# A hybrid GLA and attention step on one core: half a query tile and one gate in every head

## The chip, the core and the metric

The kernel runs on one NeuronCore of a Trainium2 chip. A core has engines that run beside each other, each with an instruction stream of its own: TensorE (PE, matrix products into PSUM), VectorE (DVE), ScalarE (ACT), GpSimd (POOL) and SyncE (SP, which here only issues DMAs). They wait for each other by semaphores, and 16 DMA engines move the data. The metric is the device time of one execution in microseconds (us); less is better.

## What is computed

One step of a two-layer backbone: layer 0 is bidirectional gated linear attention (GLA), layer 1 softmax attention with 8 query heads, 2 key/value heads and head size 128. There are 256 context tokens, which see only themselves, and 1024 latent tokens, which see all latent tokens and 256 cached context keys. The part around the change:

```python
def attn_project(h, w_in, qn, kn):
    proj = h @ w_in
    q, k, v, gate = jnp.split(proj, [ATT_QD, ATT_QD + ATT_KD, ATT_QD + 2 * ATT_KD], axis=-1)
    q = rms_norm(q.reshape(B, T, ATT_HEADS, HEAD_DIM), qn)
    ...
    def one(qblk):
        s = jnp.einsum("bqhgd,bkhd->bhgqk", qblk, keys).astype(jnp.float32) * scale
        p = jax.nn.softmax(s, axis=-1).astype(vals.dtype)
        return jnp.einsum("bhgqk,bkhd->bqhgd", p, vals)
...
        out_p = (attend_blocks(qp, kp, vp) * jax.nn.silu(gp)) @ att_w_out[i]
        ...
        xp = xp + gt_p * out_p
        xs = xs + gt_s * out_s
```

Before each layer, `h` is the RMS-normed residual stream, scaled and shifted by the conditioning; queries and keys of latent tokens get a rotary position.

## The kernel before

Every float32 product is made of two float16 parts (hi and lo) of each operand: `mm3` (L122) issues three matmuls, hi·hi, hi·lo and lo·hi, for each of the 8 blocks of 128 of the inner dimension. The 1280 tokens are 10 tiles of 128. One tile context holds the whole kernel; a scheduler in it, which simulates the engines, puts the instructions of each engine into an order of its own, close to that of the program; `issue_after(x)` says that what stands in the block comes after `x` in it.

The phases in the profiled execution are: GLA until about 557 us; the output of the GLA layer and the way into attention ("crossing") to about 736; attention to about 1177; its output projection to the end.

**Crossing**, `gla_out` (L849). For n = 2 to 9 (tiles in the order 4 to 9, then 0 and 1; two were done in the GLA phase) it makes `y = o @ w_out` into PSUM, adds it to the residual rows `x` (`residual`), and normalises, modulates and splits them (`mod_tile`, which ends with transposing DMAs into `hT_hi`, `hT_lo`, the stationary operand of the attention projections). `out_load` (L827) loads a tile of the GLA output (`og`), `out_prep` (L835) splits it into hi and lo (`oghl`) and transposes it by two DMAs that SP issues (L844, L845) into the tile's own columns of `hT_hi` and `hT_lo`, from which the matmuls of `y` read it until `mod_tile` writes there. Keys and values of attention are made beside it (`key_tile`, tile name `kv`). At n = 4 the query weights (`whi2`) are loaded by SP (L909), and at n = 8 and 9 the first two query tiles are made (`query`, `query_rest`). SP issues in order, so a transposing DMA stands behind what was issued before. PREP (L40) are slots of the GLA phase in which the first four tiles are loaded and prepared, EARLY those in which the first two are made.

**Attention**, `attention` (L1205). There are 10 steps, a pair of a key/value head p and a chunk c of 256 tokens, and 4 query heads in each, 40 heads in all. In the two steps of c = 0 (n = 4 and 6) there are 256 keys ("small"), in all others 1280 ("large"). For a head and each half j of the chunk:

- `scores` (L1091): S = q·kT into one of two PSUM tiles `S` of 3 banks (L1104, 9 matmuls for 1280 keys), its row maximum `smx` on DVE (L1107), `snb` on ACT (L1109), and p = exp on ACT (L1112), after which the bank is free.
- `rest` (L1118): the reciprocal of the sum (`srec` L1128, `srec2`), then p is normalised and split into one `phl` tile: hi on POOL for j = 0 (L1134), on ACT for j = 1 (L1136), lo on DVE (L1137). A transposing DMA by SP (L1138) takes it to `PT`. `phl` has two buffers, `PT` three.
- `gateT` (L1141): the head's gate, 24 matmuls 256 wide into a bank `mm`, emptied by ACT, then SiLU.
- `values` (L1151): v·PT, 30 matmuls for a large head, into a bank `mm`; DVE multiplies by the gate (L1162), POOL issues the store (L1163).

Queries (`queries`, L1063) are made a tile of 128 tokens and 512 columns (the four heads of p) at a time, ahead of their step: `query` (L1193) issues 24 matmuls 512 wide into a bank `mm`, takes them out by two ACT copies and finishes the norm, rotary position and transpose of two heads (`queries_out`); `query_rest` (L1201) does the other two. `mm` has two banks, shared by gates, queries, values and, at the start, `key_tile`. The queries' tiles `qT` lie in one of the two buffers `wst` of a pool for weights under way (which is why S reads `wst`); the other holds nothing in attention until the output of step n = 9 is loaded (`out2_load`, L1257).

The order of the program is: an even head makes S(j=0), a query tile, `rest`, S(j=1), and the values of the head two before; an odd head makes S(j=0), `query_rest`, values, S(j=1), then the gates of the even head and of itself, and `rest`.

**Behind it**, `out2_prep` (L1262, with `wmx`) and `out_tile` (L1280, through `residual` with banks of S) make the output projection, `fold_gate` (L807) scales its gate rows on POOL.

Of the kernel before, what the change touches and what calls it, by code (L numbers as in the profile page):

```python
# [17 lines left out]
P = 128  # L18
D = 1024
KT = D // P  # L20
TP, TS = 256, 1024
# [3 lines left out]
PAST = 256  # L25
# [13 lines left out]

PREP = (42, 44, 46, 48)  # L40
EARLY = (45, 47)
# [12 lines left out]
class K:  # L54
# [69 lines left out]
    def mm3(self, out, lhs, rhs, n=KT):  # L124
        for k in range(n):
            lh, ll = lhs(k)
            rh, rl = rhs(k)
            for j, (a, b) in enumerate(((lh, rh), (lh, rl), (ll, rh))):
                self.nc.tensor.matmul(out, a, b, start=k == 0 and j == 0, stop=k == n - 1 and j == 2)  # L129

# [695 lines left out]

    def out_load(self, i, og=None, parts=None):  # L827
        if og is None:
            og = self.og[:, i % 2]
            t = self.t(self.xp, [P, 2 * D], F16, "oghl", bufs=2)  # L830
            parts = t[:, 0:D], t[:, D:]
        self.nc.sync.dma_start(og, self.og_d[i])
        return i, og, parts
# [15 lines left out]
    def gla_out(self, wo, early, n0):  # L849
# [15 lines left out]
        for n in range(len(early), n0 + 4):  # L865
            rows[n] = self.out_load(order[n])
        ckv = self.att_load()
        for n in range(n0, NT):
            i = order[n]
            if n == NT - 1:  # L870
                self.query_rest()
                self.query()
                self.key_tile(order[n - 2], wkv)
                self.query_rest()
# [17 lines left out]
            if n == 8:  # L892
                self.query()
            if n == n0:
# [223 lines left out]
    def rest(self, after=None):  # L1118
# [11 lines left out]
        nc.vector.tensor_scalar(r2, r, 2.0 ** 14, None, ALU.mult)  # L1130
        parts = self.t(self.sp, [P, 2 * (TS + PAST)], F16, "phl")[:, 0 : 2 * nk]
        hi, lo = parts[:, 0:nk], parts[:, nk:]
# [51 lines left out]
    def query_low(self):  # L1184
# [6 lines left out]
        self.wg = [self.load_w("g0", (0, 2))]  # L1191

    def query(self):  # L1193
        if self.todo:
            p, c, j = self.todo.pop(0)
            t = self.queries(2 * c + j, *self.wq[p])
            self.half.append(t)
            self.q[(p, c, j)] = t[2]
            self.queries_out(t, 0)
# [5 lines left out]
    def attention(self, wo, wk):  # L1205
        self.S0, self.put_off = self.t(self.ps, [P, 1536], F32, "S"), None
        wq, wg, q, g = self.wq, self.wg, self.q, {}
        pend, later = [], []
        t = self.t(self.sp, [P, 20, 256], F16, "PT", bufs=3)[:, 0:16, :].rearrange("p (j k) n -> p j k n", j=2)
# [3 lines left out]
        for n, (p, c) in enumerate(self.steps):  # L1213
# [8 lines left out]
            for e in range(4):  # L1222
# [4 lines left out]
                self.scores(h, c, 0, q[(p, c, 0)], PT)  # L1227
                if e % 2 == 0:
                    self.query()
                    self.rest()  # L1230
                    self.scores(h, c, 1, q[(p, c, 1)], PT)
                else:
                    self.query_rest()
                if len(pend) == 2:
                    self.values(*pend[0], g.pop(pend.pop(0)[0]))
                else:
                    self.key_tile(len(pend), wkv)
                if e % 2 == 1:
                    self.scores(h, c, 1, q[(p, c, 1)], PT)
                pend.append((h, c, PT))  # L1240
                if e % 2 == 1:
                    g.update({i: self.gateT(i, c, *wg[p]) for i in (h - 1, h)})
                    self.rest()
                if n == 9 and e == 0:
                    row = self.out2_load(OUT[0])
                if n == 9 and e == 1:
                    first = self.ropet.rearrange("p a b d -> p (a b d)").bitcast(F16)
                    first = first.rearrange("p (j h t) -> p j h t", j=2, h=AH)
                    with self.tc.issue_after(self.last):
                        self.prep = self.out2_prep(row, (first[:, 0], first[:, 1]))  # L1250
        self.fold_gate(*self.gate_load(1), wo[0][2] + wo[1][2])
        wo[:] = [(hi, lo, 512) for hi, lo, _ in wo]
# [369 lines left out]
```

## Time and profile before

| | us |
|---|---|
| median of 3 runs | 1309.43 (1306.7 to 1311.03) |
| profiled execution | 1308.64 |
| its span | 1306.6 |
| mean granted clock of TensorE | 0.983 of full speed |
| PE idle between 560 and 1307, by the waits that ended it | 37.9 |

A page of the profile gives busy time, share of the span and number of instructions of each engine. The windows view gives the same for chosen stretches: the stretch, its length, busy time of PE, PEld (weight loads), DVE, ACT and POOL with the number of instructions in brackets, the granted clock, the share of the 16 DMA engines, GB/s. The waits view gives groups of waits of one engine: line waiting, `<-` the instruction that ended it, the sum in us, how often, the longest. A timeline row gives start, duration, engine, line, operation, result `<-` operands, sizes, and in brackets the idle time before it with what ended it; a matmul's row may stand for several in sequence (`x9`), and its duration reaches over the next one's start, so lengths are taken from start to start. Rows of SP (`SPq`) are the issuing of DMAs: how long SP stood at it, not when the data landed.

### The profile page before, as it was taken

Reading aid. Unit: us, or ns where it says so; the run is one execution under the profiler, and the core shown is the slowest. Engines: PE = TensorE matmul, PEld = TensorE weight load, DVE = VectorE, ACT = ScalarE, POOL = GpSimd, SP = SyncE. Lnnn points to the kernel's source line nnn. Section 1 sums busy time; section 2 is a strip of 40 time slices with the busy share of each in tenths; the row PEclk is TensorE's granted clock in tenths of the full one; section 3 lists DMA queues with packets and bytes.
Section 4 is the critical chain, followed back from the end, with each engine's and each line's share of the span. In section 5 each row is a group of like instructions: output and inputs, shape, how many; then the busy total and the mean of one; then the engine's idle time right before and its main releaser. Section 6 shows DMA issues by size and latency. Waiting matters only on the chain. (4 is left out here: it accounts for less than half of the span.)

```text
span 1306.6 us, 22246 instructions
## 1 busy us (share of the span) xinstructions
PE 1215.6 (93%) x7936; PEld 783.7 (60%) x7936; DVE 924.6 (71%) x2120; ACT 705.4 (54%) x1706; POOL 360.7 (28%) x594
## 2 busy tenths in 40 slices
PE   3899999999998989796999989999998999989998
PEld 2366666555645556574777557667665767766444
DVE  5575879877876798676776767777767587785652
ACT  3684656565655566541333376766766686673110
POOL 1132214223321143410223334342232345322000
PEclk9899999999998999998999999999999999999999
DMA  9712655554646343269956597666957648879342
GB/s 359 251 33 82 211 158 175 172 162 135 187 135 193 118 145 114 88 159 284 240 129 170 146 209 142 129 138 131 199 108 157 142 95 146 185 140 227 128 150 81
DMA packets 357454, 207.51 MB, mean 159 GB/s; under 512 B 251054, under 2 KB 341438, under 8 KB 354912
## 3 DMA queue, kind: packets, MB, share of 16 engines
q1 hardware_dynamic: 349824, 188.02, 56.2%
q0 software_dynamic: 4080, 12.73, 3.2%
q10 hardware_dynamic: 3440, 5.35, 1.1%
q8 instruction: 62, 1.02, 0.3%
q14 instruction: 48, 0.39, 0.1%
HBM read 107.45 MB, written 37.26 MB: 111 GB/s over the span
## 5 line engine op out<-in xcount | busy, mean ns | idle before, releaser
L129 PEld LDWEIGHTS <-hT_hi 128*128 128x128 f16 x1920 | 188.6, 98 | 133.4 <-issue 18.4
L129 PE MATMUL mm<-whi,hT_hi 128*128 128x512 f16 (+1 forms) x576 | 200.4, 348 | 13.7 <-DMA whi<-w_q 8.9
L129 PE MATMUL mm<-whi,hT_lo 128*128 128x512 f16 (+1 forms) x576 | 200.1, 347 | 0.1
L129 PE MATMUL mm<-wlo,hT_hi 128*128 128x512 f16 (+1 forms) x560 | 194.2, 347 | 0.0
L129 PEld LDWEIGHTS <-whi 128*128 128x128 f16 x1232 | 121.1, 98 | 61.3 <-issue 2.5
L1137 DVE SCALAR_TENSOR_TENSOR phl<-p,srec,phl 128x1280 f16<-128x1280 f32 (+1 forms) x80 | 108.7, 1360 | 68.5 <-POOL phl L1134 35.7
L129 PE MATMUL mm<-hT_hi,whi 128*128 128x256 f16 (+1 forms) x480 | 142.1, 296 | 0.0
L129 PE MATMUL mm<-hT_lo,whi 128*128 128x256 f16 (+1 forms) x480 | 142.0, 296 | 0.0
L129 PE MATMUL mm<-hT_hi,wlo 128*128 128x256 f16 (+1 forms) x480 | 141.9, 296 | 0.0
L129 PEld LDWEIGHTS <-hT_lo 128*128 128x128 f16 x960 | 94.5, 98 | 65.7 <-DMA hT_lo<-k 3.4
L1104 PE MATMUL S<-kT,wst 128*128 128x512 f16 (+1 forms) x624 | 122.0, 338 | 9.9 <-ACT p L1112 8.7
L129 PE MATMUL mm<-PT,vh 128*128 128x256 f16 x672 | 114.0, 275 | 11.8 <-DMA PT<-phl 8.7
L1107 DVE TENSOR_REDUCE smx<-S 128x1 f32<-128x1280 f32 (+1 forms) x80 | 101.6, 1269 | 14.3 <-PE S L1104 14.2
L1134 POOL TENSOR_SCALAR phl<-p,srec 128x1280 f16<-128x1280 f32 (+1 forms) x40 | 56.0, 1401 | 192.6 <-DVE srec L1128 77.7
L1112 ACT ACTIVATE p<-S,snb,sexp 128x1280 f32<-128x1280 f32 (+1 forms) x80 | 99.4, 1242 | 5.6 <-DVE phl L1137 1.8
L1104 PEld LDWEIGHTS <-wst 128*128 128x128 f16 x624 | 60.9, 98 | 62.3 <-issue 10.3
L129 PE MATMUL mm<-PT,vl 128*128 128x256 f16 x336 | 92.6, 276 | 0.0
L152 DVE TENSOR_REDUCE wmx<-wst 128x1 f32<-128x512 f32 x104 | 64.8, 677 | 21.2 <-DMA wst<-in_att_w_in 7.8
L129 PEld LDWEIGHTS <-vh 128*128 128x128 f16 x672 | 65.7, 99 | 23.3 <-issue 9.6
L129 PEld LDWEIGHTS <-wlo 128*128 128x128 f16 x616 | 60.6, 98 | 31.7 <-DVE wlo L1275 1.8
L942 POOL TENSOR_TENSOR rope<-hx,ropet 128x64 f32<-128x64 f32 x160 | 63.2, 425 | 30.7 <-ACT hx L1068 18.2
L1109 ACT ACTIVATE snb<-smx,nsexp 128x1 f32<-128x1 f32 x80 | 23.3, 291 | 74.9 <-DVE smx L1107 72.9
(370 smaller groups left out, 2710.2 us busy)
## 6 DMA issues: line engine op xcount, KB each, us to landing
wada<-in_w_ada SPq DMA_DIRECT2D x16, 1024.0 KB
wst<-in_gla_w_in SPq DMA_DIRECT2D x12, 1024.0 KB
wst<-in_att_w_in SPq DMA_DIRECT2D x10, 1024.0 KB
og_d<-gx SPq DMA_DIRECT2D x40, 128.0 KB
og_d<-og POOLq DMA_DIRECT2D x40, 128.0 KB, 2.8
wst<-og_d SPq DMA_DIRECT2D x5, 1024.0 KB
xr<-x_d SPq DMA_DIRECT2D x9, 512.0 KB
out<-xr ACTq DMA_DIRECT2D x17, 256.0 KB
```

Of the source, the lines that this page charges most:

```text
L129: self.nc.tensor.matmul(out, a, b, start=k == 0 and j == 0, stop=k == n - 1 and j == 2)
L152: nc.vector.tensor_reduce(mx[:, j : j + 1], st[:, 2 * j : 2 * j + 2, :], AX.XY, ALU.max, apply_absolute_value=True)
L942: nc.gpsimd.tensor_tensor(tv[:, h, :, w, :], xv[:, h, :, 1 - w, :], sn[:, :, w, :], ALU.mult)
L1104: nc.tensor.matmul(S[:, a : a + n], x, y, start=m == 0, stop=m == 2)
L1107: last = nc.vector.tensor_reduce(mx, S, AX.X, ALU.max).ins
L1109: nc.scalar.activation(nb, mx, AF.Copy, scale=self.nsexp)
L1112: nc.scalar.activation(p, S, AF.Exp, scale=self.sexp, bias=nb, accum_out=den)
L1134: nc.gpsimd.tensor_scalar(hi, p, r, 2.0 ** 14, ALU.mult, ALU.mult)
L1137: nc.vector.scalar_tensor_tensor(lo, p, r2, hi, ALU.mult, ALU.subtract)
```

## The change

Every head now makes half a query tile (`query_half`: 24 matmuls 256 wide, the first or the second two heads of the tile, an ACT copy and `queries_out` for them) between its two S, then `rest`, then the gate of the head before, then S(j=1), and then the values of the head two before. The gate and `rest` of the last head stand behind the loop. A third place for `phl` is added: the free `wst` buffer, used for every third `rest`, and given up at the end of step n = 8. In the crossing, the two `query` calls are ordered after the last matmul that `mm3` issued before them, the `og` loads of n = 4 and 5 go by POOL's queue in place of SP's, and the PREP slots are 42, 43, 45 and 46 in place of 42, 44, 46 and 48.

```diff
-PREP = (42, 44, 46, 48)
+PREP = (42, 43, 45, 46)
...
-                self.nc.tensor.matmul(out, a, b, start=k == 0 and j == 0, stop=k == n - 1 and j == 2)
+                self.pe = self.nc.tensor.matmul(out, a, b, start=k == 0 and j == 0, stop=k == n - 1 and j == 2).ins
...
-        self.nc.sync.dma_start(og, self.og_d[i])
+        (load or self.nc.sync).dma_start(og, self.og_d[i])
...
-            rows[n] = self.out_load(order[n])
+            rows[n] = self.out_load(order[n], load=nc.gpsimd)
...
-                self.query()
+                with self.tc.issue_after(self.pe):
+                    self.query()
...
-        parts = self.t(self.sp, [P, 2 * (TS + PAST)], F16, "phl")[:, 0 : 2 * nk]
+        parts = self.t(self.sp, [P, 2 * (TS + PAST)], F16, "phl") if self.turn or self.third is None else self.third
+        parts = parts[:, 0 : 2 * nk]
+        self.turn = (self.turn + 1) % 3
...
+    def query_half(self):
+        if not self.todo:
+            return
+        p, c, j = self.todo[0]
+        (hi, lo, _), inv = self.wq[p]
+        i, b = 2 * c + j, len(self.half)
+        if b == 0:
+            self.iq += 1
+            self.q[(p, c, j)] = self.qT[:, self.iq % 4]
+            self.half.append(b)
+        else:
+            self.half.pop()
+            self.todo.pop(0)
+        a = slice(256 * b, 256 * b + 256)
+        x = self.t(self.hw, [P, 4, HD], F32, "hx4")
+        ps = self.tok_proj(i, (hi[:, :, a], lo[:, :, a]), self.bank("mm")[:, 0:256])
+        xb = x[:, 2 * b : 2 * b + 2, :]
+        self.nc.scalar.activation(xb.rearrange("p h d -> p (h d)"), ps, AF.Copy, scale=inv[b])
+        self.queries_out((i, x, self.q[(p, c, j)]), b)
...
+        third = self.t(self.wst, [P, KT, 256], F32, "wst").rearrange("p k n -> p (k n)").bitcast(F16)
+        self.third, self.turn = third[:, 0 : 2 * (TS + PAST)], 0
...
-                if e % 2 == 0:
-                    self.query()
-                    self.rest()
-                    self.scores(h, c, 1, q[(p, c, 1)], PT)
-                else:
-                    self.query_rest()
+                self.query_half()
+                self.rest()
+                if pend:
+                    i, last = pend[-1][0:2]
+                    g[i] = self.gateT(i, last, *wg[i // 4])
+                self.scores(h, c, 1, q[(p, c, 1)], PT)
                 if len(pend) == 2:
                     self.values(*pend[0], g.pop(pend.pop(0)[0]))
                 else:
                     self.key_tile(len(pend), wkv)
-                if e % 2 == 1:
-                    self.scores(h, c, 1, q[(p, c, 1)], PT)
                 pend.append((h, c, PT))
-                if e % 2 == 1:
-                    g.update({i: self.gateT(i, c, *wg[p]) for i in (h - 1, h)})
-                    self.rest()
+                if n == 8 and e == 3:
+                    self.third = None
...
+        g[h] = self.gateT(h, c, *wg[p])
+        self.rest()
         self.fold_gate(*self.gate_load(1), wo[0][2] + wo[1][2])
```

More of the change, by code (lines that the diff above doesn't have):

```diff
@@ L823, in residual, with out_load @@
         return last
-    def out_load(self, i, og=None, parts=None):
+    def out_load(self, i, og=None, parts=None, load=None):
         if og is None:
@@ L892, in gla_out @@
             if n == 8:
-                self.query()
+                with self.tc.issue_after(self.pe):
+                    self.query()
             if n == n0:
@@ L1227, in attention @@
                 self.scores(h, c, 0, q[(p, c, 0)], PT)
-                if e % 2 == 0:
-                    self.query()
-                    self.rest()
-                    self.scores(h, c, 1, q[(p, c, 1)], PT)
-                else:
-                    self.query_rest()
+                self.query_half()
[4 more added lines that the diff above has]
+                self.scores(h, c, 1, q[(p, c, 1)], PT)
                 if len(pend) == 2:
```

## The prediction

> **What bounds the kernel now.** I read the page's busy shares, then PE's idle time by stage (the windows view), then what ended it (the waits view of PE, 560 to 1307 us), and only then the lines of the other engines.
>
> ```profile
> span 1306.6 us, 22246 instructions
> PE 1215.6 (93%) x7936; PEld 783.7 (60%) x7936; DVE 924.6 (71%) x2120; ACT 705.4 (54%) x1706; POOL 360.7 (28%) x594
> ```
> ```profile
> core 0: us, PE busy (x) PEld busy (x) DVE busy (x) ACT busy (x) POOL busy (x), PEclk, DMA share, GB/s
> 585.00:610.00 25.00, 22.13 (x141) 14.01 (x140) 12.15 (x30) 5.75 (x13) 3.25 (x6) 0.93 1.12 238
> 610.00:627.00 17.00, 8.10 (x58) 6.00 (x57) 13.25 (x41) 4.76 (x7) 1.70 (x3) 0.70 1.08 352
> 740.00:800.00 60.00, 51.43 (x371) 36.00 (x370) 44.05 (x76) 37.19 (x91) 20.19 (x33) 1.00 0.87 191
> 800.00:900.00 100.00, 100.00 (x707) 68.97 (x706) 72.60 (x134) 70.06 (x163) 34.50 (x57) 1.00 0.65 128
> 900.00:1090.00 190.00, 182.43 (x1308) 128.12 (x1307) 134.03 (x299) 133.11 (x353) 68.69 (x106) 0.99 0.69 142
> 1140.00:1220.00 80.00, 70.79 (x471) 46.19 (x469) 54.43 (x85) 36.74 (x66) 15.72 (x19) 0.98 0.77 175
> ```
> ```profile
> PE mm L129 <- DMA whi<-w_q: 8.9, 1, 8.9
> PE mm L129 <- ACT snb L1109: 3.1, 2, 2.1
> ```
> PE is the bound: 93% overall and 100.00 of 100 us between 800 and 900. A new order can win only what PE stands idle or runs at a lower granted clock. The idle parts are the crossing (8.9 us in one wait), the start of attention (60 - 51.43 = 8.6), its middle (190 - 182.43 = 7.6) and its end (80 - 70.79 = 9.2): some 34 us.
>
> **The change part by part.**
>
> *PREP slots and the remembered matmul.* The slots move four loads of the GLA phase; the order of each engine's instructions stays, so 0. `issue_after(self.pe)` orders PE after PE: no wait across engines, only another place in PE's order.
>
> *Crossing.* These rows, PE's and SP's in time, tell what PE waits for.
>
> ```profile
> 610.26 0.27 PE L129 MATMUL y<-wada,hT_lo 128*128 128x256 f16 x1
> 619.44 1.01 PE L129 MATMUL mm<-whi,hT_hi 128*128 128x512 f16 x2 [8.90 <-DMA whi<-w_q]
> 627.21 0.38 PE L129 MATMUL y<-whi,hT_hi 128*128 128x512 f16 x1
> 637.84 0.27 PE L129 MATMUL kv<-whi,hT_lo 128*128 128x256 f16 x1
> ```
> ```profile
> 604.86 0.92 SPq L832 DMA_DIRECT2D og<-og_d  x2
> ...
> 607.89 3.75 SPq L861 DMA_DIRECT2D xr<-in_x_sample  x1
> 611.68 0.43 SPq L909 DMA_DIRECT2D whi<-w_q  x1
> ...
> 612.69 5.62 SPq L844 DMA_TRANSPOSE hT_hi<-oghl  x1
> 618.40 4.39 SPq L845 DMA_TRANSPOSE hT_lo<-oghl  x1
> ```
> In the old order two hoisted query matmuls stand at the head of PE's queue and wait for w_q. In the new one they are gone from there, and the first matmuls of the next tile's `y` stand there; they need hT, whose two transposing DMAs SP issues from 612.69 until 618.40 + 4.39 = 622.8. What stands ahead of them on SP stays, but for the two og loads (0.92 us), which go to POOL's queue. So the wait changes its name. I estimate that PE resumes at 622.5, against 619.44. Behind that, the old stretch to 637.84 holds 18.4 us, of which 0.8 are the two query matmuls at half clock and about 1.5 the half clock's part of `kv` (granted clock 0.70 over 610 to 627); 16.1 us of work are left. With a colder array after a longer wait (half a 3.4 us stretch, 1.7) the point comes at 640.3: 2.5 later, and the two query matmuls (0.4 at full clock) still to do: **+2.9**. Bounds: if hT landed by 610.5 the whole wait and its low clock would go (8.9 + 2.3 = -11); if og came later by as much as the slowest load ahead of it (3.75), +6. I take +2.9, near the rows of SP, because the DMA share is 1.12 and 1.08 in these two windows: the transfers, not the issuing, set when hT lands.
>
> The Trainium skill, DMA: Bandwidth & Descriptors, section "Issuing engines are not separate DMA queues", says that DMAs of all issuing engines run on the same 16 engines and interleave, so another issuer saves only its sequencer's time. By that rule the moved og loads are worth their 0.92 us of SP and no more, which the full DMA share bears out; without it, the -11 of rival C would be open.
>
> *Two halves for one tile.* Widths of 256 and 512 stand side by side in PE's order:
>
> ```profile
> 862.25 0.27 PE L129 MATMUL mm<-hT_hi,whi 128*128 128x256 f16 x1
> ...
> 867.49 1.78 PE L1104 MATMUL S<-kT,wst 128*128 128x512 f16 x9
> 869.11 0.38 PE L129 MATMUL mm<-whi,hT_hi 128*128 128x512 f16 x1
> ...
> 874.29 1.79 PE L1104 MATMUL S<-kT,wst 128*128 128x512 f16 x9
> ```
> 48 matmuls 256 wide (two gates) take 867.49 - 862.25 = 5.24 us, the 24 of a whole query tile 874.29 - 869.11 = 5.18. Two halves thus cost 0.06 us more than the tile; 18 tiles: **+1.1**. ACT's two copies of a tile stay two (`queries` makes one for each half already).
>
> The Trainium skill, TensorE: Matmul & The Clock Gate, section "Back-to-back issue gap", speaks against the halves: a sustained stream of weight load and matmul is given 81 ns at 128 columns and 131 ns at 512. On a line between these, 256 columns cost an estimated 98 ns, a pair of halves 65 ns more than one whole, and 432 pairs would add an estimated 28 us. The rows above deny it for this kernel (109 and 216 ns), and fit the page's other form, N/2.4 + 2.5 ns; it gets no chance.
>
> *Order in attention.* Per head of 1280 keys PE has S 2 x 1.62 (867.49 to 869.11), half 2.62, gate 2.62 (5.24 / 2) and values 3.28 (30 matmuls at 0.109): 11.8 us, as before. What changes is the slack. From the end of a head's second S to its values, an odd head had gates 5.24 + S 1.62 + query 5.18 + S 1.62 + values 3.28 + S 1.62 = 18.6 us; now every head has twice (values + half + gate) and four S, 23.5 (22.9 in the built order). Where small heads (S 0.33: 3 matmuls 256 wide) follow, it was 5.24 + 5.18 + 3.28 + 3 x 0.33 = 14.7 and becomes 17.0 + 4 x 0.33 = 18.4. What is needed shows where PE waited for PT:
>
> ```profile
> 932.17 1.79 PE L1104 MATMUL S<-kT,wst 128*128 128x512 f16 x9
> ...
> 950.20 0.39 PE L129 MATMUL mm<-PT,vh 128*128 128x256 f16 x2 [1.24 <-DMA PT<-phl]
> ```
> ```profile
> 989.64 1.79 PE L1104 MATMUL S<-kT,wst 128*128 128x512 f16 x9
> ...
> 1009.12 0.38 PE L129 MATMUL mm<-PT,vh 128*128 128x256 f16 x2 [1.75 <-DMA PT<-phl]
> ```
> 16.2 us (950.20 - 933.96) and 17.7 us (1009.12 - 991.43). Both fit into 18.4, so the PT waits of the middle go. Of its 7.6 us I take 5.0 as gone, since the two waits for `snb` (3.1, a bank that ACT empties late) may return in part: **-5.0** (between 0 and -7.6). The granted clock of 0.99 there comes from one stretch of 3.4 us at half clock behind a 2.1 us wait; without the wait **-1.7** (or 0).
>
> The start: the first S needs exp of a bank that appears late:
>
> ```profile
> 750.89 1.78 PE L1104 MATMUL S<-kT,wst 128*128 128x512 f16 x9 [3.02 <-ACT p L1112]
> ```
> In the waits of PE from 740 to 800 two groups are of this kind:
> ```profile
> PE S L1104 <- ACT p L1112: 5.3, 2, 3.0
> PE mm L129 <- ACT rope L1055: 1.2, 1, 1.2
> ```
> With half a tile (2.6) instead of a whole before it, PE waits 5.6 instead of 3.0; the other wait for exp (5.3 - 3.0 = 2.3) and that for `rope` (1.2) should then go, less some rest of 0.4: **-0.5** (between +2.6 and -3.4). The end, waits of PE from 1140 to 1220:
> ```profile
> PE mm L129 <- DMA PT<-phl: 4.4, 3, 2.0
> PE S L1104 <- ACT p L1112: 3.2, 2, 1.9
> ```
> No query is left in the last step, so two S stand next to each other and wait for exp (3.2 of the 9.2), and values for PT (4.4). A gate between the two S covers 2.6 each; the other engines still need longer than PE there: **-3.5** (0 to -7) and half of that stage's low clock, 0.02 x 80 = 1.6: **-0.9**.
>
> *Third place.* Two phl places hold POOL back:
>
> ```profile
> POOL phl L1134 <- DMA PT<-phl: 53.5, 8, 9.3
> ```
> PE does not wait for POOL, so I price it at 0 by itself; it lets `lo`, and so PT, come earlier, which is the condition of the middle term. Late next is DVE's `lo`, behind `smx` in DVE's order. The place is a weight buffer; it is needed again only for the first output load, after the last use.
>
> **Sum** against the profiled execution (1308.64; its span 1306.6, 2.0 around it): +2.9 + 1.1 - 0.5 - 5.0 - 1.7 - 3.5 - 0.9 = -7.6, **1301.0**. That execution is 0.8 under the median of the runs shown, 1309.43, which I leave out.
>
> **The rivals.** *A, the forecast.* 1301, by its terms 1296 to 1305.
>
> *B, the gain is given back.* The crossing, the halves and the start come (+3.5), but the waits in middle and end only take other names: `mm` has two banks, now used in turn by half, gate and values, and values find theirs only gate + S = 4.2 us after the half. If ACT's copy of the half comes behind an exp that waits for `smx`, the `snb` waits grow. Half of 11.1 kept: 1308.64 + 3.5 - 5 = about 1307. For it: the `snb` row above; against it: no idle time in 800 to 900, where a gate had the same 4.2.
>
> *C, hT is ready at once.* 1301 - 2.9 - 9 = 1289. Against it: DMA share over 1.
>
> *D, the S banks, the slower side.* In the built order the next head's first S follows directly on S(h,1), ahead of values; it needs the bank of S(h,0), which ended only half + gate + S = 6.86 us before (tightest before: values + S + values = 8.2). From the end of an S to the end of its exp the old kernel took up to:
>
> ```profile
> 1110.84 1.78 PE L1104 MATMUL S<-kT,wst 128*128 128x512 f16 x9
> ...
> 1117.39 1.48 DVE L1107 TENSOR_REDUCE smx<-S 128x1 f32<-128x1280 f32 x1
> ...
> 1119.42 1.40 ACT L1112 ACTIVATE p<-S,snb,sexp 128x1280 f32<-128x1280 f32 x1
> ```
> 1120.82 - 1112.62 = 8.2 us, because `smx` began 4.8 us late. From a steady latency of 6.9 us on, PE waits once a pair; at 8.2 it is 1.34 us in each of 16 large pairs, 21 us: 1301 + 21 = 1322; where DVE catches up in these waits, 1315. For it: DVE is nearly full. Against it: what delayed `smx` is DVE's standing before `lo` for a late hi (waits of DVE, 800 to 900):
>
> ```profile
> DVE phl L1137 <- POOL phl L1134: 11.7, 8, 2.2
> DVE phl L1137 <- ACT phl L1136: 8.6, 5, 2.1
> ```
> 20.3 us in 800 to 900 beside 72.60 busy, and the third place and the new DVE order, in which `lo` stands later behind its hi, take an estimated half of it away.
>
> **How the numbers follow.** A 0.46, B 0.18, C 0.10, D 0.26. About 0.3%, 3.9 us, is what a measurement of this kernel can tell from no change: 1305.5 to 1313.4. Faster: A 0.43, C 0.10, B 0.02, together 0.55; same: A 0.03, B 0.14, D 0.02, together 0.19; slower: D 0.24, B 0.02, together 0.26. The range 1289 to 1318 holds A, B, half of C and somewhat less than half of D: 0.8. The likeliest case's own range is 1296 to 1305.
>
> **What would show it.** Crossing: one wait of 11 to 13 us before a `y` matmul, released by the DMA of hT, in place of the one for w_q. Halves: 5.24 us for two. Middle: no PE wait for PT between 900 and 1090. Third place: POOL's wait for PT under 10 us. End: 5 to 6 us idle in place of 9.2. The forecast is wrong if PE waits for exp in most pairs between 800 and 1140 (D), if PE waits for a `mm` bank (B), or if the wait at 610 is under 3 us (C).

## The result, and the profile after

The changed kernel is slower: 1317.06 us (median of 10 runs, 1310.75 to 1323.54) against 1306.59 (10 runs of the kernel before beside it; one of them, of 4446.23 us, counts as slow and stays out of the ratio), a ratio of 1.0083 with a 95% interval of 1.0064 to 1.0102. Forecast was 1301.0, faster. The time lies inside the range 1289 to 1318, close to its upper end, but it moved the other way. The profiled execution has a span of 1317.6 us and a granted clock of 0.977 (before 0.983).

The page's first part:

```profile
span 1317.6 us, 23141 instructions
PE 1219.9 (93%) x8368; PEld 825.7 (63%) x8368; DVE 927.6 (70%) x2120; ACT 706.7 (54%) x1706; POOL 373.1 (28%) x596
```

The 11.0 us that the span grew by are 4.3 of busy PE (1219.9 - 1215.6) and 6.7 of idle PE. 432 more matmuls are the halves (18 tiles x 24); the rows below show that the busy time did not grow with them, but in the output stage. Next the waits of PE from 560 us to the end (sum in us, how often, the longest):

```profile
PE y L129 <- DMA hT_hi<-oghl: 13.3, 1, 13.3
PE S L1106 <- ACT p L1114: 6.6, 5, 4.0
PE mm L129 <- DMA PT<-phl: 3.8, 3, 2.0
PE mm L129 <- DVE og L1166: 3.3, 2, 2.1
...
PE mm L87 <- DVE wm L1298: 2.6, 1, 2.6
PE S L129 <- ACT whi L1301: 2.6, 1, 2.6
...
PE mm L129 <- DMA PT<-wst: 1.3, 2, 0.9
```

Three things are to be seen. The crossing's wait changed its name as forecast, from `w_q` (8.9) to hT (13.3). The waits of attention shrank a little: PT 8.7 to 3.8 + 1.3, exp 8.7 to 6.6; the two `snb` waits (3.1) are now two waits of 3.3 for the other side of the same `mm` banks, `og` on DVE. And two waits stand at the output projection that no step of the prediction had: `wm` (2.6) and `whi` (2.6, where 1.3 for `wlo` stood).

The windows that answer to those of before (stretch, length, busy PE, PEld, DVE, ACT, POOL, granted clock, DMA share, GB/s), and behind them the whole of attention and the output stage, cut as described below:

```profile
743.00:800.00 57.00, 48.67 (x366) 36.40 (x365) 40.86 (x70) 32.42 (x76) 19.22 (x28) 0.94 0.90 198
800.00:900.00 100.00, 98.09 (x803) 78.20 (x801) 73.16 (x131) 69.82 (x161) 42.82 (x59) 1.00 0.69 128
900.00:1090.00 190.00, 186.16 (x1571) 153.17 (x1569) 140.45 (x304) 136.89 (x360) 66.53 (x105) 1.00 0.68 138
1140.00:1212.00 72.00, 66.06 (x478) 46.27 (x476) 49.94 (x80) 39.77 (x74) 17.71 (x24) 1.00 0.84 200
743.16:1217.04 473.88, 451.29 (x3634) 355.42 (x3632) 345.48 (x658) 314.48 (x749) 168.11 (x244) 0.99 0.75 155
1217.04:1313.15 96.11, 92.06 (x430) 42.87 (x429) 41.09 (x66) 6.67 (x6) 0.00 (x0) 0.95 0.35 117
```

and of before the last two:

```profile
736.23:1213.36 477.13, 451.79 (x3202) 313.63 (x3200) 340.82 (x658) 312.65 (x749) 159.16 (x244) 0.99 0.73 153
1213.36:1302.23 88.87, 87.59 (x431) 41.93 (x429) 40.78 (x65) 6.67 (x6) 0.00 (x0) 1.00 0.37 129
```

Idle PE is length minus busy: 8.3 at the start of attention (8.6 before), 1.9 from 800 to 900 (0 before), 3.8 in the middle (7.6 before) and 5.9 at its end (9.2 before). These windows do not hold quite the same work: 1.1 of the 1.9 us is a wait for the DMA of the queries that before has, with 0.9, at 796 us, and the 2.57 us wait for `whi` lies behind the end's window, where before's window has its 1.33. Cut at the same matmuls, attention's idle time falls only from 25.3 to 22.6 us, and that of the output stage rises from 1.3 to 4.0. Attention's busy time is the same with 432 matmuls more (451.8 and 451.3). In the output stage the same work takes 4.5 us more of busy time (92.06 against 87.59), at a granted clock of 0.95 against 1.00.

To compare kernels whose phases shift, I cut every trace at the same matmuls. **Crossing**: from the end of the last `y` matmul of the tiles n = 2 and 3 to the first weight matmul of the next tile's `kv`; the work between them is equal, but for the two query matmuls in the kernels marked W. **Attention**: from the last `y` matmul's start to that of the 430th matmul before the end. **Output**: from there to the last matmul's start. A ratio is to the kernel before, run beside it; the three stretches come from one profiled execution of each kernel. W, y and kv in the last column tell what PE has first in the crossing: the two query matmuls that wait for `w_q`, the `y` of n = 4, or `kv`.

| kernel | ratio (95%) | crossing | attention | output | PE order |
|---|---|---|---|---|---|
| before | 1 | 27.1 | 477.1 | 88.9 | W |
| changed | 1.0083 (1.0064 to 1.0102) | 30.8 | 473.9 | 96.1 | y |
| e5, changed again | 1.0070 (1.0044 to 1.0095) | 31.2 | 475.4 | 92.3 | y |
| e1, crossing only | 1.0026 (1.0007 to 1.0046) | 30.8 | 475.0 | 88.8 | y |
| e2, attention only | 1.0014 (0.9992 to 1.0036) | 28.4 | 474.8 | 93.2 | W |
| e3, query order only | 0.9996 (0.9971 to 1.0021) | 25.2 | 477.1 | 88.7 | kv |
| e4, changed, og on SP | 0.9995 (0.9973 to 1.0016) | 26.8 | 476.6 | 90.2 | kv |
| e6, halves, two places | 1.0156 (1.0127 to 1.0185) | 29.5 | 494.3 | 93.2 | W |
| e7, e3 with a late w_q | 0.9975 (0.9953 to 0.9996) | 26.2 | 473.3 | 88.6 | kv |
| e8, e4 with a late w_q | 1.0010 (0.9989 to 1.0032) | 25.7 | 473.3 | 93.7 | kv |
| e9, changed, kv first | 1.0001 (0.9987 to 1.0014) | 23.9 | 477.2 | 93.3 | kv |
| e10, third place only | 1.0052 (1.0029 to 1.0074) | 27.0 | 481.3 | 92.9 | W |
| e11, e7 with third place | 1.0022 (0.9999 to 1.0045) | 27.3 | 482.5 | 89.5 | kv |
| e12, e4, split first | 0.9991 (0.9972 to 1.0010) | 25.6 | 473.4 | 91.1 | kv |
| e13, e9 shifted | 1.0005 (0.9982 to 1.0028) | 23.9 | 476.2 | 91.1 | kv |
| e14, before shifted | 1.0008 (0.9994 to 1.0023) | 26.3 | 476.2 | 92.3 | W |

### The profile page after: what moved, and what is told of

It is laid out like the page before. It is cut to its first block, busy times and chain, and to the rows that moved or that the text cites. A ratio compares the mean times of both kernels' runs of the same rounds, so it can differ in the third digit from the quotient of the medians.

```text
span 1317.6 us, 23141 instructions
## 1 busy us (share of the span) xinstructions
PE 1219.9 (93%) x8368; PEld 825.7 (63%) x8368; DVE 927.6 (70%) x2120; ACT 706.7 (54%) x1706; POOL 373.1 (28%) x596
## 3 DMA queue, kind: packets, MB, share of 16 engines
q1 hardware_dynamic: 349536, 186.97, 55.9%
## 5 line engine op out<-in xcount | busy, mean ns | idle before, releaser
L129 PEld LDWEIGHTS <-hT_hi 128*128 128x128 f16 x2208 | 217.4, 99 | 111.8 <-DMA hT_hi<-oghl 13.6
L129 PE MATMUL mm<-whi,hT_hi 128*128 128x256 f16 (+1 forms) x720 | 225.2, 313 | 2.4 <-ACT gx L562 2.0
L129 PE MATMUL mm<-whi,hT_lo 128*128 128x256 f16 (+1 forms) x720 | 224.9, 312 | 0.0
L129 PE MATMUL mm<-wlo,hT_hi 128*128 128x256 f16 (+1 forms) x704 | 219.0, 311 | 0.1
L129 PEld LDWEIGHTS <-hT_lo 128*128 128x128 f16 x1104 | 108.7, 98 | 52.3 <-DMA hT_lo<-k 3.5
L1106 PE MATMUL S<-kT,wst 128*128 128x512 f16 (+1 forms) x624 | 124.4, 341 | 10.5 <-ACT p L1114 6.6
L1141 DVE SCALAR_TENSOR_TENSOR phl<-p,srec,phl 128x1280 f16<-128x1280 f32 (+1 forms) x56 | 79.2, 1425 | 31.7 <-ACT phl L1140 17.0
L944 POOL TENSOR_TENSOR rope<-hx,ropet 128x64 f32<-128x64 f32 x160 | 77.3, 511 | 28.1 <-ACT hx L1215 16.0
L129 PEld LDWEIGHTS <-wlo 128*128 128x128 f16 x616 | 60.6, 98 | 30.8 <-issue 1.9
L120 POOL TENSOR_TENSOR hrs<-hrsa,mhalf 128x2 f32<-128x2 f32 x50 | 42.3, 847 | 79.7 <-DVE hrsa L118 79.6
```

Source lines behind the costliest of these rows:

```text
L120: nc.gpsimd.tensor_tensor(r, a, self.mhalf[:, 0:w], ALU.pow)
L129: self.pe = self.nc.tensor.matmul(out, a, b, start=k == 0 and j == 0, stop=k == n - 1 and j == 2).ins
L944: nc.gpsimd.tensor_tensor(tv[:, h, :, w, :], xv[:, h, :, 1 - w, :], sn[:, :, w, :], ALU.mult)
L1106: nc.tensor.matmul(S[:, a : a + n], x, y, start=m == 0, stop=m == 2)
L1141: nc.vector.scalar_tensor_tensor(lo, p, r2, hi, ALU.mult, ALU.subtract)
```

## The experiments: the two halves of the change

**e1** is the kernel before with the crossing's edits, **e2** the kernel before with attention's.

```diff
# e1
-PREP = (42, 44, 46, 48)
+PREP = (42, 43, 45, 46)
+            rows[n] = self.out_load(order[n], load=nc.gpsimd)
+                with self.tc.issue_after(self.pe):
+                    self.query()
# e2
+                self.query_half()
+                self.rest()
...
+        self.third, self.turn = third[:, 0 : 2 * (TS + PAST)], 0
```

> The kernel before with the crossing's edits alone (PREP slots, query ordered after the last matmul, og loads of n = 4 and 5 on POOL's queue); attention as before. Theory 1 (the crossing costs): the moved og loads let the scheduler put the first matmuls of the next y ahead of kv, PE stands about 13 us at hT_hi instead of 8.9 at w_q, and the kernel is 4 to 7 us slower than before, 1310 to 1314. Theory 2 (attention or its tail costs, the crossing's stretch is only a matter of the one profiled execution): 1305 to 1308.

> The kernel before with the attention's edits alone (half a query tile and one gate in every head, third place for phl). Theory 1 (only the crossing costs; attention gains the 2 us that the trace shows up to the last values): 1303 to 1306. Theory 2 (the new order of attention costs, by S banks or by the output stage behind it, where the trace shows 6 us): 1311 to 1316.

Measured: 1311.27 us, +0.26% (0.07 to 0.46), and 1308.99, +0.14% (-0.08 to 0.36). The crossing alone costs what was forecast for it (2.9 us are 0.22%). Attention's edits, forecast at -10.5 us (the sum without the crossing), bring nothing that can be measured; the time lies between the two ranges that were expected. **e5** ran the changed kernel a second time, with no edit.

> The changed kernel itself once more, timed beside the other runs. Apart, the crossing's edits cost 0.26% and the attention's 0.14%, together 0.40%; the change was measured at 0.83%. Theory 1 (the parts add): 0.2 to 0.6% slower, 1309.5 to 1314, so that the first figure was high. Rival (they cost more together than apart): again 0.64 to 1.0%, 1315 to 1320, with more idle time of PE in one stage than either part has by itself.

Measured: 1315.64, 1.0070 (1.0044 to 1.0095); the loss stands. The sum of e1 and e2 is 0.40%, which lies just below e5's interval: the parts together seem to cost some 0.3% more than one by one. With 0.2% of uncertainty in each of e1 and e2 this is not sure.

## The experiments: the crossing

**e3** keeps only `issue_after`; **e4** is the changed kernel without the new queue for `og`:

```diff
# e3, on the kernel before
+                with self.tc.issue_after(self.pe):
+                    self.query()
# e4, on the changed kernel
-            rows[n] = self.out_load(order[n], load=nc.gpsimd)
+            rows[n] = self.out_load(order[n])
```

> The kernel before with one edit: the two query calls ordered after the last matmul before them. PE's order then has kv, not y, behind the first tiles. Theory 1 (what counts is what stands first in PE's order): kv (5.4 us) runs into the wait, y waits for hT until about 623 us instead of starting at 627.2, and the time is 3 to 5 us under that of before, 1301.5 to 1304. Rival (the transfers bind, so any order ends at the same point): 1305.5 to 1308.

> The changed kernel with the two og loads back on SP's queue, all else as changed. PE's order in the crossing is that of the query order alone (kv before y). Theory 1: the crossing's loss goes and becomes a gain of some 4 us against before, and attention adds 2: 1299 to 1304. Theory 2 (attention costs): 1308 to 1313.

Measured: 1306.20, 0.9996, and 1307.07, 0.9995. Neither gained the 3 us or more of its theory 1: e3 lies in the rival's range, although its crossing is 1.9 us shorter than before's, and e4 between its two ranges. One line, the queue of two loads, carries the loss between e4 and the changed kernel. PE's rows in time, of the changed kernel first and then of e3, show what it did:

```profile
626.62 0.61 PE L129 MATMUL y<-whi,hT_hi 128*128 128x512 f16 x1 [13.30 <-DMA hT_hi<-oghl]
...
633.21 0.39 PE L87 MATMUL kv<-ident,amx 128*128 128x128 bf16 x4
```
```profile
616.24 0.29 PE L87 MATMUL kv<-ident,amx 128*128 128x128 bf16 x1 [6.93 <-DVE amx L1001]
```

In the changed kernel `y` of n = 4, which needs hT, stands ahead of `kv` in PE's order, and `kv`, which needs only `amx` from DVE, waits behind it until 633.21. In e3 `kv` stands first and fills the time in which hT lands. The scheduler decides this place; with the loads on POOL's queue it puts `y` in front.

Is it the queue or the order? **e9** leaves the loads on POOL and holds `y` of n = 4 behind the last `kv` matmul:

```diff
-            last = self.residual(i, lambda k: (hT[:, k, :], lT[:, k, :]), wo, inv, x)
+            with ExitStack() as order_y:
+                if n == 4:
+                    order_y.enter_context(self.tc.issue_after(self.pe))
+                last = self.residual(i, lambda k: (hT[:, k, :], lT[:, k, :]), wo, inv, x)
```

> The changed kernel, og loads still on POOL's queue, with the y of n = 4 ordered after the last matmul of kv, so that PE's order in the crossing is kv before y again. Theory 1 (PE's order is what the crossing costs, not the queue of the og loads): the stretch from first to last y falls from 156 to 159 us to about 150 to 152, and the time is 3 to 6 us under the changed kernel's, ratio to before 1.003 to 1.006. Rival (the og loads come too late from POOL's queue): the stretch stays over 155 and the ratio stays at 1.006 to 1.009.

Measured: 1306.83, 1.0001 (0.9987 to 1.0014). PE's rows of e9:

```profile
618.31 0.29 PE L87 MATMUL kv<-ident,amx 128*128 128x128 bf16 x1 [6.15 <-DVE amx L1004]
...
625.24 0.38 PE L129 MATMUL y<-whi,hT_hi 128*128 128x512 f16 x1
...
626.05 0.39 PE L129 MATMUL y<-whi,hT_lo 128*128 128x512 f16 x1 [0.21 <-DMA hT_lo<-oghl]
```

The wait of 13.30 became 6.15 + 0.21, and `y` follows on `kv` with no wait for the first part of hT. The crossing shrank by 30.8 - 23.9 = 6.9 us, and the loss against before went: more than the 3 to 6 us expected, and 2 to 4 us more than the crossing gave. The traces of e9 and e4 have all their matmuls in the same order, with the loads on POOL in one and on SP in the other, and their ratios are 1.0001 and 0.9995. So the queue by itself costs nothing that can be measured; the cost is in PE's order. The order differs from the changed kernel's at 78 matmuls of the crossing, but also at 634 of attention between 792 and 961 us. Attention takes 473.9 and 475.4 us in the changed kernel's two traces and 477.2 and 476.6 in e9's and e4's, so these traces show no loss there. By orders, the crossing takes 30.9 us with y first (3 kernels), 27.6 with W (5) and 25.1 with kv first (5, without e7, e8, e11).

**e7** (on e3) and **e8** (on e4) also move SP's load of `w_q` behind the two transposing DMAs of n = 4:

```diff
+            if n == n0:
+                first = self.tr
-                nc.sync.dma_start(self.q0, self.ahead["q0"][0][:, 0])
+                with self.tc.issue_after(first):
+                    nc.sync.dma_start(self.q0, self.ahead["q0"][0][:, 0])
```

> The kernel before with the query calls ordered after the last matmul, and the load of w_q issued by SP behind the two transposing DMAs of the next tile instead of ahead of them. Theory 1 (in the crossing PE waits for hT, and hT for the bytes that SP has issued ahead of it): hT lands 4 to 5 us earlier, y starts near 619 us, and the kernel is 3 to 5 us faster than before, 1302 to 1305. Rival (the whole stretch is bound by the DMA engines, any order only moves the wait to the next tile): same as with the query order alone, 1305 to 1308.

> The changed kernel with the og loads on SP and w_q behind the transposing DMAs. Theory 1 (crossing as in the run before it; the attention order worth nothing to within 2 us): 1301 to 1306. Rival (attention's order and the output stage behind it cost 2 us or more): 1306 to 1310.

Measured: 1303.66, 0.9975 (0.9953 to 0.9996), and 1309.46, 1.0010. SP's rows of the changed kernel, then of e7 (issuing only):

```profile
614.45 0.43 SPq L911 DMA_DIRECT2D whi<-w_q  x1
...
615.45 6.71 SPq L844 DMA_TRANSPOSE hT_hi<-oghl  x1
622.25 3.18 SPq L845 DMA_TRANSPOSE hT_lo<-oghl  x1
```
```profile
609.86 3.14 SPq L844 DMA_TRANSPOSE hT_hi<-oghl  x1
613.09 4.13 SPq L845 DMA_TRANSPOSE hT_lo<-oghl  x1
...
617.90 0.56 SPq L914 DMA_DIRECT2D whi<-w_q  x1
```

In e7 the transposes are issued earlier: the second one's issue ends 11.5 us behind the crossing's start (617.22 - 605.75), where the changed kernel has 12.1 (625.43 - 613.32) and e3 12.5 (621.85 - 609.31). That could gain nothing: with `kv` first, `y` follows on `kv` without a wait for hT in e3 already. Nor does `y` start earlier: 15.8 us behind the crossing's start in e7 (621.54), 14.7 in e3 (624.04). So e7's time lies in the range of theory 1, but its mechanism did not happen. e7's crossing is not shorter than e3's (26.2 against 25.2); e8's is 1.1 us shorter than e4's, and e8, in the rival's range, is not faster. e7 is the fastest version run, and the only one whose interval lies under 1; that the late load is the reason is not shown.

## The experiments: attention

**e6** is e2 without the third place, with the same order on PE; **e10** is the kernel before with the third place alone, **e11** is e7 with it.

```diff
# e6, on e2
-        parts = self.t(self.sp, [P, 2 * (TS + PAST)], F16, "phl") if self.turn or self.third is None else self.third
+        parts = self.t(self.sp, [P, 2 * (TS + PAST)], F16, "phl")
# e10, on the kernel before; e11, on e7
-        parts = self.t(self.sp, [P, 2 * (TS + PAST)], F16, "phl")[:, 0 : 2 * nk]
+        parts = self.t(self.sp, [P, 2 * (TS + PAST)], F16, "phl") if self.turn or self.third is None else self.third
```

> The attention's edits without the third place for phl (two phl buffers as before); crossing as before; the order of PE is the same as with the place. Theory 1 (the place takes waits from POOL alone, which PE does not see): same time as the attention's edits with it, 1306 to 1311. Rival (the place is what makes PT early): waits of PE for PT return, each 1 to 2 us at some 10 places, 1315 to 1325.

> The kernel before with the third place for phl alone; queries and gates as before. With the halves the place was worth 1.4% (1.0156 without it, 1.0014 with it). Theory 1 (the place helps wherever POOL waits for PT, 46 us before): PE's waits for PT between 900 and 1090 and at the end shrink from 8.7 to under 4 us and the kernel is 3 to 6 us faster, ratio 0.995 to 0.998. Rival (only the order with halves needs it, since it asks for phl earlier): ratio 0.998 to 1.002.

> The kernel before with the query calls ordered after the last matmul, w_q behind the transposing DMAs, and the third place for phl. If both parts gain by themselves: 0.993 to 0.996. If the place gains nothing in the old order: as the first two alone, 0.996 to 0.999.

Measured: e6 1329.19, 1.0156; e10 1315.26, 1.0052; e11 1310.01, 1.0022. The third place, priced at 0 by itself, is worth 1.4% under the new order (1.0156 against 1.0014; attention 494.3 and 474.8). With the old program order the kernels that have it are about 0.5% slower (1.0052 against 1; 1.0022 against 0.9975; attention 481.3 and 482.5, where those without it have 473.3 to 477.1); none of the ranges expected for e10 and e11 held that. Waits of PE from 740 to 1225 in e6, and then in e10:

```profile
PE mm L129 <- DVE og L1163: 9.8, 7, 2.3
PE mm L129 <- ACT hx L1212: 5.3, 2, 3.8
PE mm L129 <- DMA PT<-phl: 3.2, 4, 1.4
```
```profile
PE mm L129 <- DMA PT<-phl: 11.0, 4, 4.5
```

and POOL's wait for PT (740 to 1220) in e6, in e10 and in the changed kernel:

```profile
POOL phl L1135 <- DMA PT<-phl: 55.9, 13, 6.4
```
```profile
POOL phl L1136 <- DMA PT<-phl: 26.8, 3, 13.1
```
```profile
POOL phl L1138 <- DMA PT<-phl: 25.1, 5, 6.4
```

With two places the new order waits for `mm` banks (9.8 + 5.3 us) and not, as the rival expected, mainly for PT (3.2 us): the halves and gates share the two banks with values, and DVE and ACT, which empty them, also work on phl. DVE's waits for the hi parts of phl are 71.1 us in e6 and 44.3 in e2 (740 to 1220); that this is what holds the banks up is argued, not tested. The third place about halves POOL's wait in either order (from 55.9 to 22.5 in e2, from 53.5 in before to 26.8 in e10), and in the new one PE has that time back.

e2 and e6 have all their matmuls in the same order, so this pair compares the place alone. The other two pairs do not: with the place the scheduler puts other matmuls at 272 places of PE's order in e10 than in before, and at the same 272 in e11 than in e7. The attention of e7 and of e11:

```profile
730.99:1204.30 473.31, 448.56 (x3202) 312.04 (x3200) 341.53 (x659) 312.71 (x749) 158.68 (x244) 1.00 0.74 154
732.13:1214.61 482.48, 456.76 (x3203) 316.12 (x3201) 343.96 (x659) 314.23 (x749) 160.43 (x244) 0.98 0.74 152
```

Idle time is 24.8 us and 25.7; what grew is the busy time for the same matmuls, by 8.2 us, at a granted clock of 0.98 against 1.00. All runs say the same: the clock granted over a whole run is 0.985 on average in e7's runs and 0.980 in e11's, 0.983 in the runs of before beside them and 0.979 in e10's. A difference of 0.0045 in 1307 us is an estimated 5.9 us, close to the 6.4 between e7 and e11 (1303.66 and 1310.01). So by these figures what is lost in the old order is mostly clock and not waiting. Why the clock is granted less there is not shown.

## The experiments: the output stage

All nine kernels with halves take 90.2 to 96.1 us there; before, e1, e3 and e7 take 88.6 to 88.9, but e10, e11 and e14, also without halves, 92.9, 89.5 and 92.3. Two waits differ. The first is PE's wait for the split of the first output tile. By the cuts above it still belongs to attention (the output stage begins at 1213.36 in before and at 1217.04 in the changed kernel). These are the matmul with which the split's chain begins, and the wait, of before and then of the changed kernel:

```profile
1208.07 0.22 PE L87 MATMUL mm<-ident,wm 128*128 128x128 bf16 x1
...
1212.70 0.39 PE L129 MATMUL S<-whi,wlo 128*128 128x512 f16 x1 [1.33 <-DVE wlo L1275]
```
```profile
1212.72 0.22 PE L87 MATMUL mm<-ident,wm 128*128 128x128 bf16 x1
...
1215.94 0.39 PE L129 MATMUL S<-whi,whi 128*128 128x512 f16 x1 [2.57 <-ACT whi L1301]
```

It is 1.3 us in all seven kernels with whole query tiles, and 2.6 in all eight with halves that keep DVE's order. PE's order goes with it. Behind the matmul at L87, DVE and ACT make the scale and the split; meanwhile PE has other matmuls to do, 11 of them in all seven kernels with whole tiles and only 2 in all nine with halves. **e12** (on e4) puts DVE's scaling of the first output tile behind the split:

```diff
+            with ExitStack() as order:
+                if after is not None:
+                    order.enter_context(self.tc.issue_after(after))
+                nc.vector.scalar_tensor_tensor(ps, ps, inv, g[:, a], ALU.mult, ALU.mult)
+                last = nc.vector.tensor_tensor(x[:, a], ps, x[:, a], ALU.add).ins
```

> The changed kernel with the og loads on SP and, in the output stage, DVE's scaling of the first tile of att_out ordered behind the split of the next chunk. Theory 1 (DVE's order there, the tile's S ahead of p2, makes the split late): PE's first wait of the stage falls from 2.57 to 1.3 us or less, the stage from last values to the end of PE from 95.7 to 98 to about 94.5, the time 1 to 2 us under that without this edit (0.9995). Rival (the stage is long because of its loads, at the third chunk): the stage stays over 95.5.

Measured: 0.9991, not apart from e4. The wait for `whi` shrank by 0.5, but 0.3 came back:

```profile
1205.01 0.58 PE L129 MATMUL S<-whi,whi 128*128 128x512 f16 x1 [2.04 <-ACT whi L1304]
```

(and 0.31 for `wlo` behind it). The edit did what it says: DVE's scaling, which stood inside the chain, stands behind it, and from L87 to `whi` it is 2.69 us and not 3.22. So DVE's order is a small part of the wait, and PE's order, which e12 leaves alone there, the likely rest; no run changed that. The second wait is for `wm`, the maximum of the last chunk of output weights, whose load (issued by SP at L1286) lands late. The load's issue, DVE's reduction of it and PE's wait in the changed kernel, then the first two in the kernel before:

```profile
1250.11 0.92 SPq L1286 DMA_DIRECT2D wst<-og_d  x1
...
1258.86 2.35 DVE L1294 TENSOR_REDUCE wmx<-wst 128x1 f32<-128x1024 f32 x2 [7.84 <-DMA wst<-og_d]
...
1261.99 0.29 PE L87 MATMUL mm<-ident,wm 128*128 128x128 bf16 x1 [2.63 <-DVE wm L1298]
```
```profile
1244.97 0.32 SPq L1259 DMA_DIRECT2D wst<-og_d  x1
...
1250.67 2.34 DVE L1267 TENSOR_REDUCE wmx<-wst 128x1 f32<-128x1024 f32 x2 [4.68 <-DMA wst<-og_d]
```

From issue to use it is 8.75 us (1258.86 - 1250.11) against 5.70. In the record of DMA packets one of 16 KB begins 0.63 us before that load's issue; before has none near it. It is on a queue that none of the kernel's own transfers uses and that the page of the profile lists as `q8 instruction`, with 65 packets for 16736 PE instructions (a matmul and a weight load each), one in about 257. I took it for a fetch of PE's program, whose place the 864 added PE instructions move. **e13** (on e9) and **e14** (on before) move it by small transposes at the start of PE's program, whose result is overwritten:

```diff
+        for _ in range(40):   # e13; 54 in e14
+            nc.tensor.transpose(ps[:, 0:32], self.ident[0:32, :], self.ident[0:32, 0:32])
```

> The changed kernel with kv ahead of y (ratio 1.0001), and 40 transposes of a constant ahead of PE's first instruction, whose result nothing reads; no other order changes. Theory (the instruction packet of PE falls on the load of the last chunk by the number of PE's instructions ahead of it): the packet comes some 4 to 9 us earlier than the load, the load lands in about 5.7 us, PE's wait for wm (2.8 us) goes, and the last 430 matmuls take about 90.5 us instead of 93.3. Rival (the load is slow by what the stage moves): load over 8 us, stage over 92.5.

> The kernel before with 54 transposes of a constant ahead of PE's first instruction; no other order changes but a few of DVE's at the start. In its output stage the packet stood 11.4 us behind the load's issue. Theory: it now falls on the load, which lands after 8 to 9 us instead of 5.7, PE waits 1.5 to 3 us for wm, and the last 430 matmuls take 91 to 93 us instead of 88.7. If a transpose is one instruction and not two, it falls between and the stage stays at 88.7. Rival: 88.5 to 89 wherever the packet falls.

Measured: 1.0005 (e9 1.0001) and 1.0008 (0.9994 to 1.0023). The packet went where it was sent: in e14 to 1.13 us before the load, in e13 to 6.2 us before it, so far off. DVE's reduction and PE's wait in e14, then in e13:

```profile
1251.05 2.35 DVE L1269 TENSOR_REDUCE wmx<-wst 128x1 f32<-128x1024 f32 x2 [7.42 <-DMA wst<-og_d]
...
1254.18 0.23 PE L87 MATMUL mm<-ident,wm 128*128 128x128 bf16 x1 [2.19 <-DVE wm L1273]
```
```profile
1252.40 2.35 DVE L1299 TENSOR_REDUCE wmx<-wst 128x1 f32<-128x1024 f32 x2 [6.75 <-DMA wst<-og_d]
...
1255.53 0.23 PE L87 MATMUL mm<-ident,wm 128*128 128x128 bf16 x1 [1.53 <-DVE wm L1303]
```

e14 did what the packet's theory said: the old kernel's load takes 8.35 us instead of 5.70, the new wait appears, and the stage is 3.4 us longer. e13 did not: the packet is gone, SP's issue is short again (0.32 us, after 1.02 in e9), but the load still takes 8.12 us, and e10 has 8.33 without any packet there. So the packet goes with the long issue; a slow load comes with it and without it, each time seen in one execution, and the packet is not its only cause. The other one stays open. How much of it is in the medians is open too: e14's allows -0.8 to +3.0 us.

## Why the prediction was wrong

*Crossing, +2.9: right.* The wait before `y` by the DMA of hT came (13.3 us, a little over the 11 to 13 that were named), and the stretch with y first is 30.9 us against 27.6, +3.3. What the step took for given is that `y` must stand there. It asked when hT lands and not what else PE could do meanwhile; `kv`, one place behind, had 5.4 us of work (633.21 to 638.57), 6.9 in e9 at a lower clock. So rival C, that hT is ready at once, was the wrong way to think of a gain here: in e9 the order covers it.

The Trainium skill, DMA: Bandwidth & Descriptors, section "Issuing engines are not separate DMA queues", was weighed there: another issuer saves its sequencer's time at most. The trace agrees: with the `og` loads off SP, its issue of the second transpose still ends 12.1 us behind the crossing's start, against 12.3 before (622.79 - 610.53).

*Halves, +1.1: right.* Rows of the changed kernel, the starts of the two halves and of the S behind them:

```profile
864.83 0.27 PE L129 MATMUL mm<-whi,hT_hi 128*128 128x256 f16 x1
...
867.45 0.27 PE L129 MATMUL mm<-hT_hi,whi 128*128 128x256 f16 x1
...
870.07 1.24 PE L1106 MATMUL S<-kT,wst 128*128 128x512 f16 x5
```

A stretch of 24 matmuls takes 2.62 us, two 5.24.

*Start -0.5, middle -5.0 and -1.7, end -3.5 and -0.9: this is the step that failed.* The step forecast 9.0 us less idle time and 2.6 less for lower clock. In the profiled execution some waits went where it looked: the middle's idle time fell by 3.8 (7.6 to 3.8). But attention as a whole lost only 2.7 us of it (25.3 to 22.6), and its clock stayed at 0.99. PT was still waited for (3.8 + 1.3 us, of it 2.3 in the middle, where none was forecast), and `mm` banks for 3.3, as rival B had it; 1.2 us came with the wait for `whi`. At the start the first wait for exp is 3.99 (5.6 forecast, 3.02 before), and between 800 and 900, where PE never stood, it now stands before S for exp, twice:

```profile
758.09 3.36 PE L1106 MATMUL S<-kT,wst 128*128 128x512 f16 x9 [3.99 <-ACT p L1114]
...
872.21 1.02 PE L1106 MATMUL S<-kT,wst 128*128 128x512 f16 x4 [0.35 <-ACT p L1114]
...
896.38 0.81 PE L1106 MATMUL S<-kT,wst 128*128 128x512 f16 x3 [0.49 <-ACT p L1114]
```

That is rival D's place at a third of its price, 0.35 to 0.49 instead of 1.34. The start's clock fell to 0.94. Over all kernels, attention takes 475.1 us in the new order (8 kernels with the third place) and 475.8 in the old one (5 without it): -0.7 against a forecast of -10.5 with the halves; single traces of either kind lie between 473.3 and 477.2. That is rival B's outcome, the gain given back, for attention; its time for the kernel, 1307, lacks what the output stage lost. The step took every idle stretch as a gain of its own. But the change gave DVE and ACT no less work (their busy time in attention, 340.8 and 312.7 us, became 345.5 and 314.5), and for most of the waits that went, others stand at other banks and places. That the one brought the other is read from the waits views, and no run tested it wait by wait.

*Third place, 0 by itself: wrong.* In the new order it saves 1.4% of the time; with the old one the kernels that have it are 0.5% slower, with another order of PE and a lower clock. POOL's wait for PT was to be under 10 us and is 25.1. The price of 0 was argued from PE, which does not wait for POOL; but the `mm` banks that it waits for in e6 are emptied by DVE and ACT, which share the work on phl with POOL.

*Output stage, no term: +3.9* (92.7 on average with halves, 88.7 in before, e1, e3 and e7): 2.4 us of idle time, most of it the wait for `wm` behind the late load, and 1.5 of longer busy time at a lower clock (in the profiled execution 2.8 and 4.5). Nothing in the diff touches this stage's program, so the prediction passed it over. How much of it belongs to the halves is open, since e10 without halves has 92.9.

*Sum.* By the stretches, +3.3 - 0.7 + 3.9 = +6.5 us; measured are +10.5 (ratio interval 8.4 to 13.3 us) and in e5 +9.2 by its ratio (5.8 to 12.4). What is left, some 3 to 4 us, is open. Part of it may be clock: over a whole run the changed kernel is granted 0.980 on average, here and in e5, and before 0.983 in the runs beside e5, an estimated 4 us of 1310, part of which is in the stretches already. Another candidate is the GLA phase: the crossing starts at 610.8 on average in the eight kernels with the new PREP slots and at 608.8 in the eight without, but single ones lie between 604.6 and 613.8 in both groups together, so it is not shown.

## What to carry to other kernels

When a load is moved to another queue under a scheduler, compare the engines' orders and not only the landing time: here two loads on POOL put `y` ahead of `kv`, 7 us on PE, and one ordering line took it back. The same holds for a buffer: the third place moved 272 matmuls in one order and none in the other. Idle time of the bound engine inside a steady loop is no sum of separate gains: here the engines beside it kept their work, and PE's idle time in attention fell by 2.7 us where 9.0 were forecast; so test each edit with and without the buffer that it leans on. And give a stage behind the change its own term when what runs into it changes.

## What the runs showed of the hardware

In the profiled execution of e14, 54 small transposes at the start of PE's program went with a load 1240 us later that took 8.35 us in place of before's 5.70; a 16 KB packet of the queue `q8 instruction` stood 1.13 us before it. That the packet slowed the load is not shown: e10 and e13 have 8.33 and 8.12 us with none so near. SP's issue of that load took 0.9 to 1.4 us, in place of 0.32, in the six kernels whose packet began 0.3 to 0.65 us ahead of it, and 0.32 in the other ten.

Two kernels with the same matmuls, partly in another order, and nearly the same idle time (24.8 and 25.7 us) differ by the clock that they were granted: PE's busy time in attention is 448.6 us in e7 and 456.8 in e11, at 1.00 and 0.98.
